# Two-block transformer layer on one core: the row tiles placed 192 bytes past the weight pieces, modulo 256

## The chip, the cores and the metric

One NeuronCore of a Trainium2 chip runs the whole program. The metric is the device time of one execution in microseconds (us); the runs of the kernel before took 2258.59 to 2259.89 us, median 2259.46.

## What is computed

Two transformer blocks in float32, one after the other, on 256 tokens of width 2048. Nearly all arithmetic is in dense projections of the kind "activations times weight matrix":

```python
# block 1
h = rms_norm(x, mix_norm_g);  proj = h @ w_in
attn = nsa_attention(q, kv, gates, ...)        # compressed, selected and window branches
conv = conformer_conv(conv_in, ...)            # GLU, 31-tap depthwise conv, LayerNorm, swish
x = x + concat([attn, conv]) @ w_out
x = x + conv_glu_ffn(rms_norm(x, ffn_norm_g), w_up, ffn_conv_w, ffn_conv_b, w_down)
x = rms_norm(x, final_norm_g)
# block 2
ada = silu(c) @ w_ada + b_ada                  # six modulation vectors
z = (rms_norm(x) * (1 + scale_m) + shift_m) @ w_in_2
o = concat([mla_mixer(...), gla_mixer(...)]) @ w_out_2
x = x + gate_m * rms_norm(o)
f = (silu(h @ w_ffn_gate) * (h @ w_ffn_up)) @ w_ffn_down   # h: modulated rms_norm of x
return x + gate_f * rms_norm(f)
```

## The kernel before, in words

**Every projection is done as three products.** Weights and activations are float32, but the tensor engine is used in its float32r form. So each operand is split in a rounded high part and the remainder as a low part, and the product is taken as high*high + high*low + low*high. The activations are kept transposed, 128 channels on the partitions and 256 tokens along the row; such a 128 x 256 piece, and its low part, are what is called **rows** here. The weights stream in from memory: a DMA brings 1 MB into `raw`, ScalarE writes the high part into a `wh` buffer, VectorE the low part into a `wl` buffer (`split_h`, `split_l`, lines 456 to 475). There are four `wh` and three `wl` buffers of 128 x 1024 elements (4096 bytes per partition), cut into pieces of 128 x 128 (512 bytes per partition).

**The matmuls** are issued by `run_group` (line 551). In most groups (mode "w") a weight piece is the stationary operand and the rows move: per piece and channel block three matmuls of 256 columns, (high weights, high rows), (high weights, low rows), (low weights, high rows), each with a weight load of its own. In groups of mode "x" the rows are stationary, in slices of 128 tokens, and 512 weight columns move. In the profile the two operands of a matmul stand after the arrow, the moving one first: "X,wh" is a matmul of mode "w", "wh,hid" one of mode "x".

**Where rows live.** `xsrc` gives the main rows: the high parts `XH` (16 blocks at a distance of 384 elements) and the low parts `XL` (16 blocks of 256) in one tile `X`. Other groups read: `o` (attention output, two times 8 blocks), `ch` and `cl` (convolution output, high and low), `hid` (hidden rows of both feed-forward stages), `cqs`, `ckh`, `ckl` (the compressed queries and keys of the second block), and `oh0`..`oh7`, `ol0`..`ol7` (its attention output, which reuse the space of the `qn` and `kn` tiles). `rows()` (line 707) makes the tiles `X`, `o` and `hid`, and before the change it skips `PHASE` = 4 elements, 16 bytes, at the front of each.

**Where a tile lies** follows from the order in which tiles are asked for in a pool, and of the pools: each takes its size, rounded up to 32 bytes per partition. The pool `cp` (`setup`) comes first with `XT`, `adaT`, `gf`, `X`, `vecs`, `kc`, `cs`, `gs`; then `rp` (nine tiles of 1024 bytes), the three `raw` buffers of 8192 bytes, the seven `wh` and `wl` buffers, and behind them the pools of each stage (`b1`, `f1`, `b2o` with `b2`, `f2`).

**The order of the work** is written by a small model of the engines in the kernel: `run_group` issues a group's matmuls and, between them, work of other engines and small matmuls from generators (`side`, `tick`) when the model holds them to be due. Neither addresses nor paddings enter this model. One such generator is `ada_gen`, which now and then puts eight small float32 matmuls and one transpose between the row matmuls.

All compute instructions are issued by one wrapper and so show as line 305 in the profile; they are told apart by the names of their tiles.

Of the kernel before, what the change touches and what calls it, by code (L numbers as in the profile page):

```python
# [13 lines left out]
F32 = mybir.dt.float32  # L14
F32R = mybir.dt.float32r
# [8 lines left out]
T = 256  # L24
# [122 lines left out]
WARM = 8  # L147
SQ = 1
AHEAD = 2
PHASE = 4  # L150
XROW = 384
GROUPS, MCS, TILES, WLEN = make_plan()

# [26 lines left out]
class Layout:  # L180
    def __init__(self, items):
        self.at, o = {}, 0
        for k, n in items:
# [12 lines left out]
CB = Layout([("perm", 128), ("selA", 128), ("selB", 128), ("cm3", 384), ("glam", 128), ("rmask", 256), ("invf", 1),  # L196
             ("sgn", 1), ("wgu", 512)])
# [175 lines left out]
class Kern:  # L373
# [330 lines left out]

        self.act(self.kc[:, 3:4], self.eps, AF.Sqrt)

    def rows(self, pool, name, parts, skip=PHASE):


        t = pool.tile([128, skip + sum(n * w for n, w in parts)], F32R, name=name)  # L710
        out, o = [], skip
        for n, w in parts:
            out.append(t[:, o:o + n * w].rearrange("p (k t) -> p k t", t=w))
            o += n * w
        return out
# [48 lines left out]
    def setup(self):  # L764
        a = self.a
        self.XT = self.cp.tile([128, 16, T], F32, name="XT")
        self.adaT = self.cp.tile([128, 96], F32, name="adaT")
        self.gf = self.cp.tile([128, 16], F32, name="gf")
        self.XH, self.XL = self.rows(self.cp, "X", ((16, XROW), (16, T)))
        self.vecs = self.cp.tile([128, VEC.n], F32, name="vecs")  # L770
        self.kc = self.cp.tile([128, 4], F32, name="kc")
        self.cs = self.cp.tile([128, 16], F32, name="cs")
        self.gs = self.cp.tile([128, 16], F32, name="gs")
        self.v.memset(self.kc[:, 0:1], EPS)
        self.v.memset(self.kc[:, 1:2], 1.0)
        self.v.memset(self.kc[:, 2:3], float(np.pi / 2))
        self.eps, self.one, self.hpi = self.kc[:, 0:1], self.kc[:, 1:2], self.kc[:, 2:3]
        self.ident = self.vec("ident", 0, 128)
        self.ones = self.vec("ones", 0, 128)
        self.begin(*(g["key"] for g in GROUPS if g["w"] == "w_in"))  # L780
        self.no_rows()


    def block1_setup(self):
        tc, a, ph = self.tc, self.a, self.ph
        self.p1 = ph.enter_context(ExitStack())
        P = self.b1 = self.p1.enter_context(tc.tile_pool(name="b1", bufs=1))
        self.oh, self.ol = self.rows(P, "o", ((8, T), (8, T)))
        self.cacc = [P.tile([128, 4, T], F32, name=f"cacc{b}") for b in range(2)]
        self.cat = P.tile([128, CA.n], F32, name="cat")  # L790
        self.sy.dma_start(self.cat[:, :16], a["ca"][:, :16])
        self.cl = {}
        self.upad = P.tile([128, 8, 30 + T], F32, name="upad")
        self.kz = P.tile([128, 4, 2, T], F32, name="kz")
        self.V = P.tile([128, 2, 2, 4, 64], F32, name="V")
        self.Gt = P.tile([128, 2, 8, 2, 3], F32, name="Gt")
        self.cbias = P.tile([128, 2, 8, 2, 16], F32, name="cbias")
        self.kcz = P.tile([128, 4, 16], F32, name="kcz")
        self.vz = P.tile([128, 4, 64], F32, name="vz")
        self.qT = {}  # L800
        self.pe1 = self.p1.enter_context(ExitStack())
        Ep = self.early = self.pe1.enter_context(tc.tile_pool(name="early", bufs=1))
        g = self.gp
        g.memset(self.upad[:, :, 0:30], 0.0)
        g.memset(self.kz, 0.0)
        g.memset(self.kcz, 0.0)
        g.memset(self.vz, 0.0)
        g.memset(self.cbias, NEG)
        for i in range(4):
            self.evac[f"c{i}"] = lambda ps, i=i: self.ev_conv(i, ps)  # L810
            self.evac[f"q{i}"] = lambda ps, i=i: self.ev_q(i, ps)
        for i in range(8):
            self.evac[f"oa{i}"] = lambda ps, i=i: self.ev_add([2 * i, 2 * i + 1], ps)
            self.evac[f"ob{i}"] = self.evac[f"oa{i}"]
            self.evac[f"oz{i}"] = lambda ps, i=i: self.ev_oz([2 * i, 2 * i + 1], ps)
        self.evac["kvc"] = self.ev_kvc
        self.evac["kk"] = self.ev_kk
        self.evac["gt"] = self.ev_gt
        self.evac["vv"] = self.ev_vv

        z = self.cacc[0][:, 0]
        self.v.memset(z, 0.0)
        o = self.bank()
        for _ in range(WARM):
            self.mm(o[:, :T], z[:, :128], z)
        self.free(o)
        for n, (c0, c1) in enumerate(((0, 2), (2, 4), (4, 8))):
            self.load_x(c0, c1)
            self.load_raw(n + 1)
        self.load_x(8, 12)  # L830
        g = lambda k: self.ca("mix_g", k)
        self.feed_raw(range(2), g)
        self.side(self.first_gen(g))
        self.conv_side = self.side(self.conv_gen(), low=True)
        self.side(self.bias_gen())
        self.ffn1_evacs()
        self.block2_evacs()
# [51 lines left out]
    def conv_gen(self):  # L889
        up, ca = self.upad, self.cacc  # L890
        for i in range(4):
# [14 lines left out]
                self.tt(up[:, 0:2, 0:T], ca[0][:, 0:2], ca[0][:, 2:4], OP.add)  # L906
            elif i > 1:
                self.tt(up[:, 0:2, 0:T], up[:, 0:2, 0:T], y, OP.add)
        self.ch = self.b1.tile([128, 8, T], F32R, name="ch", tag="ch")
        yield  # L910
        yield from self.need(1)
        o = self.sums([up[:, 0, 0:T], up[:, 1, 0:T]])
# [317 lines left out]
    def pre_u0_0(self):  # L1230
        self.idles = 0
        while "att" not in self.flags:
            self.idle()
        self.p1.close()
        self.p2 = self.ph.enter_context(ExitStack())
        P = self.f1 = self.p2.enter_context(self.tc.tile_pool(name="f1", bufs=1))
        self.begin("u0_0")
        self.side(self.norm_gen(lambda k: self.fv[:, 352 + k:353 + k]))
        self.hh, self.hl_ = self.rows(P, "hid", ((22, T), (22, T)))
        self.fv = P.tile([128, FV.n], F32, name="fv")  # L1240
        self.sy.dma_start(self.fv, self.a["fv"])
        self.vt = [P.tile([128, 4, 2 + T], F32, name=f"vt{i}") for i in range(2)]
        for t in self.vt:
            self.gp.memset(t[:, :, 0:2], 0.0)
        self.act(self.cs, self.vec("c", 0, 16), AF.Silu)
        self.ada_side = self.side(self.ada_first(P))
# [131 lines left out]
    def pre_z0(self):  # L1378
        self.drain(self.ada_side)
        self.p2.close()  # L1380
        P3 = self.p3 = self.ph.enter_context(ExitStack())
        Po = P3.enter_context(self.tc.tile_pool(name="b2o", bufs=1))
        self.b2o = Po
        self.qn, self.kn = ([Po.tile([128, T + PHASE], F32, name=f"{n}{h}")[:, PHASE:] for h in range(8)] for n in ("qn", "kn"))
        self.omh, self.oml = {}, {}
        self.gg = Po.tile([128, 128], F32, name="gg")[:, :16]
        self.p3i = P3.enter_context(ExitStack())
        P = self.b2 = self.p3i.enter_context(self.tc.tile_pool(name="b2", bufs=1))
        self.cbt = P.tile([128, CB.n], F32, name="cbt")
        self.sy.dma_start(self.cbt, self.a["cb"])  # L1390
        self.tt(self.gg, self.adaT[:, 32:48], self.vec("g_post", 0, 16), OP.mult)
        self.begin("z0", "z1")
        self.norm2_side = self.side(self.norm2_gen())
        self.cos = P.tile([128, T], F32, name="cos")
        self.sin = P.tile([128, T], F32, name="sin")
        self.qg = P.tile([128, 4, T], F32, name="qg")
        self.kg = P.tile([128, 4, T], F32, name="kg")
        self.sr = P.tile([128, 8, T], F32, name="sr")
        self.Vg = self.Vm = None
        self.krz = P.tile([128, 2, T], F32, name="krz")  # L1400
        self.zkr = P.tile([128, T], F32, name="zkr")
        self.dec = P.tile([128, 4, 4], F32, name="dec")
        self.kdz = P.tile([128, 3, 128], F32, name="kdz")
        for t in (self.krz, self.kdz):
            self.gp.memset(t, 0.0)
        self.side(self.rope_gen())
        self.ada_side = self.side(self.ada_late(P))
# [76 lines left out]
        self.side(self.rms_gen(c, 4, "g_q", self.cqh, self.cql))  # L1484

    def ev_shift(self, dst, ps, scales=(1, 1, 1, 1)):
        sh = self.b2.tile([128, 4], F32, name="sh", bufs=2)
        for e, (d, p, s) in enumerate(zip(dst, ps, scales)):
            self.shift(sh[:, e:e + 1], p, s)
            self.tt(d, p[:, :T], self.R, OP.mult)  # L1490
        for e, (d, s) in enumerate(zip(dst, scales)):
            self.act(d, d, AF.Identity, bias=sh[:, e:e + 1], scale=s)
# [129 lines left out]
    def mla_gen(self, h):  # L1622
# [27 lines left out]
        while self.pt_busy:  # L1650
# [17 lines left out]
        self.mm(o[:, 128:T], self.Vm[:, 1, hs], PT[:, 256:], False, True)  # L1668
        self.pt_busy = False
        yield  # L1670
        oh, ol = (self.b2o.tile([128, T + PHASE], F32R, name=f"{n}{h}", tag=f"{t}{h}")[:, PHASE:]
                  for n, t in (("oh", "qn"), ("ol", "kn")))
        self.omh[h], self.oml[h] = oh, ol
        self.act(oh, o[:, :T], AF.Copy)
# [354 lines left out]
```

## Time and profile before

| | us |
|---|---|
| median of 3 runs (2258.59 to 2259.89) | 2259.46 |
| the profiled execution | 2265.83 |
| its span, first to last instruction | 2263.9 |
| TensorE busy (PE) in it | 2234.7 |
| weight loads (PEld) | 2137.7 |
| VectorE (DVE) | 1698.5 |
| ScalarE (ACT) | 1187.7 |
| mean granted clock of TensorE, of full speed | 0.996 |

The profiled execution took 6.37 us more than the median run. Busy times are the union of an engine's instructions. Matmuls overlap each other in the records (one starts before the end of the one before it), so how fast they follow is read from how many of them stand in a stretch, not from the mean length of one.

### The profile page before, as it was taken

Reading aid. Unit: us, or ns where it says so; the run is one execution under the profiler, and the core shown is the slowest. Engines: PE = TensorE matmul, PEld = TensorE weight load, DVE = VectorE, ACT = ScalarE, POOL = GpSimd, SP = SyncE. Lnnn points to the kernel's source line nnn. Section 1 sums busy time; section 2 is a strip of 40 time slices with the busy share of each in tenths; the row PEclk is TensorE's granted clock in tenths of the full one; section 3 lists DMA queues with packets and bytes.
Section 4 is the critical chain, followed back from the end, with each engine's and each line's share of the span. In section 5 each row is a group of like instructions: output and inputs, shape, how many; then the busy total and the mean of one; then the engine's idle time right before and its main releaser. Section 6 shows DMA issues by size and latency. Waiting matters only on the chain.

```text
span 2263.9 us, 42338 instructions
## 1 busy us (share of the span) xinstructions
PE 2234.7 (99%) x17486; PEld 2137.7 (94%) x17486; DVE 1698.5 (75%) x2632; ACT 1187.7 (52%) x1826; POOL 4.9 (0%) x16
## 2 busy tenths in 40 slices
PE   8999999999999999999999999999999999999997
PEld 8998889999999999999999889989998999889996
DVE  7999888898987788888879876577665665544455
ACT  5447776655553355555556664555444444444443
POOL 0000000000000000000000000000000000000000
PEclk9999999999999999999999999999999999999999
DMA  6544325688888787877756644546666665555553
GB/s 242 186 166 159 127 80 193 239 293 301 303 287 308 294 297 284 301 291 290 251 204 225 214 153 148 193 149 215 241 239 231 246 236 192 187 183 171 187 186 130
DMA packets 89089, 499.22 MB, mean 221 GB/s; under 512 B 9904, under 2 KB 12352, under 8 KB 42432
## 3 DMA queue, kind: packets, MB, share of 16 engines
q1 hardware_dynamic: 88896, 496.51, 61.7%
q8 instruction: 137, 2.24, 0.4%
q14 instruction: 56, 0.46, 0.1%
HBM read 494.35 MB, written 2.12 MB: 219 GB/s over the span
## 4 chain that ended last, share of the span: by engine, by line
PE 93%; DVE 4%; ACT 2%; issue 1%; DMA 1%; SPq 0%; DVEq 0%; ACTq 0%
PE ps L305 93%; DVE wl L305 1%; DMA raw<-in_wst_dram 1%; DVE cacc L305 0%; ACT wh L305 0%; DVE og L305 0%; ACT P L305 0%; DVE X L305 0%; ACT X L305 0%; ACT L305 0%; DVE ss L305 0%; DVE blk L305 0%; ACT y L305 0%; ACT vt L305 0%; DVE XT L305 0%
## 5 line engine op out<-in xcount | busy, mean ns | idle before, releaser
L305 PE MATMUL ps<-X,wh 128*128 128x256 f32 (+1 forms) x7680 | 1374.8, 281 | 3.6 <-ACT X L305 2.9
L305 ACT ACTIVATE wh<-raw 128x1024 fp32r<-128x1024 f32 (+2 forms) x741 | 781.5, 1056 | 875.6 <-PE ps L305 798.8
L305 DVE TENSOR_TENSOR wl<-raw,wh 128x1024 fp32r<-128x1024 f32 (+2 forms) x741 | 898.5, 1216 | 451.4 <-PE ps L305 381.3
L305 PEld LDWEIGHTS ps<-X,wh 128*128 128x128 f32 x7680 | 1174.5, 188 | 12.3 <-issue 5.8
L305 PE MATMUL ps<-X,wl 128*128 128x256 f32 (+1 forms) x3840 | 1073.8, 280 | 3.4 <-DVE wl L305 3.4
L305 PEld LDWEIGHTS ps<-X,wl 128*128 128x128 f32 x3840 | 721.3, 188 | 4.0 <-DVE wl L305 4.0
L305 DVE SCALAR_TENSOR_TENSOR ac<-wa,cs,ac 128x512 f32<-128x512 f32 x360 | 269.6, 749 | 6.4
L305 PE MATMUL ps<-hid,wh 128*128 128x256 f32 x1408 | 247.8, 279 | 0.0
L305 PE MATMUL ps<-wh,hid 128*128 128x512 f32 x704 | 220.1, 394 | 0.0
L305 PEld LDWEIGHTS ps<-hid,wh 128*128 128x128 f32 x1408 | 214.1, 188 | 1.2 <-issue 1.2
L305 PE MATMUL ps<-hid,wl 128*128 128x256 f32 x704 | 196.0, 278 | 0.0
L305 PEld LDWEIGHTS ps<-wh,hid 128*128 128x128 f32 x704 | 131.7, 188 | 29.2 <-issue 0.2
L305 PE MATMUL ps<-wl,hid 128*128 128x512 f32 x352 | 138.1, 392 | 0.0
L305 PEld LDWEIGHTS ps<-hid,wl 128*128 128x128 f32 x704 | 132.2, 188 | 0.0
L305 DVE SCALAR_TENSOR_TENSOR cacc<-upad,cat,cacc 128x256 f32<-128x256 f32 x240 | 99.7, 478 | 0.3 <-ACT cacc L305 0.2
L305 PEld LDWEIGHTS ps<-wl,hid 128*128 128x128 f32 x352 | 67.1, 191 | 15.7
L305 DVE SCALAR_TENSOR_TENSOR y<-vt,fv,y 128x256 f32<-128x256 f32 x176 | 73.4, 479 | 0.0
L305 PE MATMUL ps<-wh,X 128*128 128x512 f32 x192 | 62.0, 404 | 0.0
L305 PE MATMUL ps<-o,wh 128*128 128x256 f32 x256 | 48.9, 290 | 1.2 <-ACT o L305 1.1
L305 ACT ACTIVATE y<-ps,fv 128x256 f32<-128x256 f32 x84 | 49.0, 583 | 0.0
L305 ACT ACT_TABLE_LOAD x30 | 38.5, 1283 | 10.8 <-DMA XT<-in_x_dram 4.5
L305 PEld LDWEIGHTS ps<-wh,X 128*128 128x128 f32 x192 | 35.4, 189 | 7.3
(319 smaller groups left out, 1754.8 us busy)
## 6 DMA issues: line engine op xcount, KB each, us to landing
raw<-in_wst_dram SPq DMA_DIRECT2D x363, 1024.0 KB, 4.9
wa<-in_wada_dram SPq DMA_DIRECT2D x176, 512.0 KB, 6.2
wa<-in_wada_dram SPq DMA_DIRECT2D x32, 256.0 KB, 5.5
raw<-in_wst_dram SPq DMA_DIRECT2D x4, 768.0 KB, 4.4
raw<-in_wst_dram SPq DMA_DIRECT2D x4, 512.0 KB, 6.3
B<-dtab SPq DMA_DIRECT2D x8, 256.0 KB, 5.2
out_dram<-og SPq DMA_DIRECT2D x8, 256.0 KB, 2.8
XT<-in_x_dram SPq DMA_DIRECT2D x3, 512.0 KB, 7.5
```

The source lines that it names most:

```text
L305: return f(*x, **k)
```

## The change

The constant `PHASE` is replaced by `SKIP` = 48 elements (192 bytes), which `o` and `hid` now skip, while `X` skips nothing; in `setup` the tiles `X` and `vecs` are asked for after `kc`, `cs` and `gs`. `ch` is asked for at the start of `block1_setup`, behind `cacc`. `gg` is made 192 bytes long and put ahead of `qn` and `kn`, which lose their skip (and so do `oh` and `ol`). `cbt`, `dec` and `sh` are made longer, with only their first part used. No instruction is added, removed or moved to another place in an engine's order.

```diff
--- before.py
+++ after.py
@@ -147,7 +147,7 @@
 WARM = 8
 SQ = 1
 AHEAD = 2
-PHASE = 4
+SKIP = 48
 XROW = 384
 GROUPS, MCS, TILES, WLEN = make_plan()
 
@@ -704,7 +704,7 @@
 
         self.act(self.kc[:, 3:4], self.eps, AF.Sqrt)
 
-    def rows(self, pool, name, parts, skip=PHASE):
+    def rows(self, pool, name, parts, skip=0):
 
 
         t = pool.tile([128, skip + sum(n * w for n, w in parts)], F32R, name=name)
@@ -766,11 +766,11 @@
         self.XT = self.cp.tile([128, 16, T], F32, name="XT")
         self.adaT = self.cp.tile([128, 96], F32, name="adaT")
         self.gf = self.cp.tile([128, 16], F32, name="gf")
-        self.XH, self.XL = self.rows(self.cp, "X", ((16, XROW), (16, T)))
-        self.vecs = self.cp.tile([128, VEC.n], F32, name="vecs")
         self.kc = self.cp.tile([128, 4], F32, name="kc")
         self.cs = self.cp.tile([128, 16], F32, name="cs")
         self.gs = self.cp.tile([128, 16], F32, name="gs")
+        self.XH, self.XL = self.rows(self.cp, "X", ((16, XROW), (16, T)))
+        self.vecs = self.cp.tile([128, VEC.n], F32, name="vecs")
         self.v.memset(self.kc[:, 0:1], EPS)
         self.v.memset(self.kc[:, 1:2], 1.0)
         self.v.memset(self.kc[:, 2:3], float(np.pi / 2))
@@ -785,8 +785,9 @@
         tc, a, ph = self.tc, self.a, self.ph
         self.p1 = ph.enter_context(ExitStack())
         P = self.b1 = self.p1.enter_context(tc.tile_pool(name="b1", bufs=1))
-        self.oh, self.ol = self.rows(P, "o", ((8, T), (8, T)))
+        self.oh, self.ol = self.rows(P, "o", ((8, T), (8, T)), SKIP)
         self.cacc = [P.tile([128, 4, T], F32, name=f"cacc{b}") for b in range(2)]
+        self.ch = P.tile([128, 8, T], F32R, name="ch")
         self.cat = P.tile([128, CA.n], F32, name="cat")
         self.sy.dma_start(self.cat[:, :16], a["ca"][:, :16])
         self.cl = {}
@@ -906,7 +907,6 @@
                 self.tt(up[:, 0:2, 0:T], ca[0][:, 0:2], ca[0][:, 2:4], OP.add)
             elif i > 1:
                 self.tt(up[:, 0:2, 0:T], up[:, 0:2, 0:T], y, OP.add)
-        self.ch = self.b1.tile([128, 8, T], F32R, name="ch", tag="ch")
         yield
         yield from self.need(1)
         o = self.sums([up[:, 0, 0:T], up[:, 1, 0:T]])
@@ -1236,7 +1236,7 @@
         P = self.f1 = self.p2.enter_context(self.tc.tile_pool(name="f1", bufs=1))
         self.begin("u0_0")
         self.side(self.norm_gen(lambda k: self.fv[:, 352 + k:353 + k]))
-        self.hh, self.hl_ = self.rows(P, "hid", ((22, T), (22, T)))
+        self.hh, self.hl_ = self.rows(P, "hid", ((22, T), (22, T)), SKIP)
         self.fv = P.tile([128, FV.n], F32, name="fv")
         self.sy.dma_start(self.fv, self.a["fv"])
         self.vt = [P.tile([128, 4, 2 + T], F32, name=f"vt{i}") for i in range(2)]
@@ -1381,13 +1381,13 @@
         P3 = self.p3 = self.ph.enter_context(ExitStack())
         Po = P3.enter_context(self.tc.tile_pool(name="b2o", bufs=1))
         self.b2o = Po
-        self.qn, self.kn = ([Po.tile([128, T + PHASE], F32, name=f"{n}{h}")[:, PHASE:] for h in range(8)] for n in ("qn", "kn"))
+        self.gg = Po.tile([128, SKIP], F32, name="gg")[:, :16]
+        self.qn, self.kn = ([Po.tile([128, T], F32, name=f"{n}{h}") for h in range(8)] for n in ("qn", "kn"))
         self.omh, self.oml = {}, {}
-        self.gg = Po.tile([128, 128], F32, name="gg")[:, :16]
         self.p3i = P3.enter_context(ExitStack())
         P = self.b2 = self.p3i.enter_context(self.tc.tile_pool(name="b2", bufs=1))
-        self.cbt = P.tile([128, CB.n], F32, name="cbt")
-        self.sy.dma_start(self.cbt, self.a["cb"])
+        self.cbt = P.tile([128, -(-CB.n // 64) * 64], F32, name="cbt")
+        self.sy.dma_start(self.cbt[:, :CB.n], self.a["cb"])
         self.tt(self.gg, self.adaT[:, 32:48], self.vec("g_post", 0, 16), OP.mult)
         self.begin("z0", "z1")
         self.norm2_side = self.side(self.norm2_gen())
@@ -1399,7 +1399,7 @@
         self.Vg = self.Vm = None
         self.krz = P.tile([128, 2, T], F32, name="krz")
         self.zkr = P.tile([128, T], F32, name="zkr")
-        self.dec = P.tile([128, 4, 4], F32, name="dec")
+        self.dec = P.tile([128, 64], F32, name="dec")[:, :16].rearrange("p (h n) -> p h n", h=4)
         self.kdz = P.tile([128, 3, 128], F32, name="kdz")
         for t in (self.krz, self.kdz):
             self.gp.memset(t, 0.0)
@@ -1484,7 +1484,7 @@
         self.side(self.rms_gen(c, 4, "g_q", self.cqh, self.cql))
 
     def ev_shift(self, dst, ps, scales=(1, 1, 1, 1)):
-        sh = self.b2.tile([128, 4], F32, name="sh", bufs=2)
+        sh = self.b2.tile([128, 32], F32, name="sh", bufs=2)
         for e, (d, p, s) in enumerate(zip(dst, ps, scales)):
             self.shift(sh[:, e:e + 1], p, s)
             self.tt(d, p[:, :T], self.R, OP.mult)
@@ -1668,7 +1668,7 @@
         self.mm(o[:, 128:T], self.Vm[:, 1, hs], PT[:, 256:], False, True)
         self.pt_busy = False
         yield
-        oh, ol = (self.b2o.tile([128, T + PHASE], F32R, name=f"{n}{h}", tag=f"{t}{h}")[:, PHASE:]
+        oh, ol = (self.b2o.tile([128, T], F32R, name=f"{n}{h}", tag=f"{t}{h}")
                   for n, t in (("oh", "qn"), ("ol", "kn")))
         self.omh[h], self.oml[h] = oh, ol
         self.act(oh, o[:, :T], AF.Copy)
```

## Rows read from the trace of the kernel before

**Rows 1.** The page, parts 1 and 2: PE's share, the granted clock.

```profile
PE 2234.7 (99%) x17486; PEld 2137.7 (94%) x17486; DVE 1698.5 (75%) x2632; ACT 1187.7 (52%) x1826; POOL 4.9 (0%) x16
...
PEclk9999999999999999999999999999999999999999
```

**Rows 2.** The page, part 4: the chain that ended last, by engine.

```profile
PE 93%; DVE 4%; ACT 2%; issue 1%; DMA 1%; SPq 0%; DVEq 0%; ACTq 0%
```

**Rows 3.** The page, part 5: matmuls that read rows, and the weight split.

```profile
L305 PE MATMUL ps<-X,wh 128*128 128x256 f32 (+1 forms) x7680 | 1374.8, 281 | 3.6 <-ACT X L305 2.9
...
L305 DVE TENSOR_TENSOR wl<-raw,wh 128x1024 fp32r<-128x1024 f32 (+2 forms) x741 | 898.5, 1216 | 451.4 <-PE ps L305 381.3
...
L305 PE MATMUL ps<-X,wl 128*128 128x256 f32 (+1 forms) x3840 | 1073.8, 280 | 3.4 <-DVE wl L305 3.4
...
L305 PE MATMUL ps<-hid,wh 128*128 128x256 f32 x1408 | 247.8, 279 | 0.0
L305 PE MATMUL ps<-wh,hid 128*128 128x512 f32 x704 | 220.1, 394 | 0.0
...
L305 PE MATMUL ps<-hid,wl 128*128 128x256 f32 x704 | 196.0, 278 | 0.0
...
L305 PE MATMUL ps<-wl,hid 128*128 128x512 f32 x352 | 138.1, 392 | 0.0
```

**Rows 4.** Busy time by stretch, PE alone: from:to length, PE busy (matmuls), clock, DMA, GB/s.

```profile
399.00:476.00 77.00, 77.00 (x652) 1.00 0.71 255
...
1540.00:1655.00 115.00, 115.00 (x973) 1.00 0.65 230
...
sum 515.00, PE 515.00; mean PE 64.38
```

**Rows 5.** The same view, other stretches.

```profile
478.50:1004.00 525.50, 524.86 (x4538) 1.00 0.82 297
...
sum 712.50, PE 711.86; mean PE 142.37
```

**Rows 6.** The same view, three neighbouring stretches of one stage.

```profile
967.00:1003.00 36.00, 36.00 (x311) 1.00 0.85 309
1008.00:1040.00 32.00, 32.00 (x285) 1.00 0.79 289
1043.00:1083.00 40.00, 40.00 (x345) 1.00 0.81 297
```

**Rows 7.** The same view: the stage that reads ch and cl.

```profile
352.00:388.00 36.00, 36.00 (x310) 1.00 0.56 197
```

**Rows 8.** The same view: stages with 512 weight columns moving.

```profile
1690.00:1735.00 45.00, 45.00 (x194) 1.00 0.69 243
...
2195.00:2240.00 45.00, 45.00 (x201) 1.00 0.48 165
```

**Rows 9.** Groups of instructions by line, 364 to 380 us, PE.

```profile
L305 PE MATMUL ps<-ch,wh 128*128 128x256 f32 x47 | 13.1, 279 | 0.0
L305 PE MATMUL ps<-cl,wh 128*128 128x256 f32 x46 | 12.9, 280 | 0.0
L305 PE MATMUL ps<-ch,wl 128*128 128x256 f32 x46 | 12.8, 278 | 0.0
```

**Rows 10.** Groups by line, 404 to 420 us and then 1014 to 1030 us, PE.

```profile
L305 PE MATMUL ps<-X,wh 128*128 128x256 f32 x92 | 16.4, 280 | 0.0
...
L305 PE MATMUL ps<-X,wh 128*128 128x256 f32 x60 | 10.2, 276 | 0.0
```

**Rows 11.** Timeline of PE around 1006 us: start, length, work, count.

```profile
1006.10 0.33 PE L305 MATMUL ps<-vecs,ac 128*128 128x128 f32 x1 [0.35 <-ACT ac L305]
1006.19 0.48 PE L305 MATMUL ps<-X,wh 128*128 128x256 f32 x2
```

**Rows 12.** One tile's instructions: what writes ol (eight places in SBUF).

```profile
L305 DVE TENSOR_TENSOR ol<-ps,oh x8: 398/418/425, 1273.7 to 1338.6; 128x256 fp32r<-128x256 f32 x8
```

**Rows 13.** Busy time by stretch, all engines: PE, PEld, DVE, ACT, POOL busy.

```profile
540.00:600.00 60.00, 60.00 (x523) 59.34 (x522) 54.83 (x76) 32.17 (x45) 0.00 (x0) 1.00 0.82 295
```

## The prediction

> **What bounds the kernel now.** I read the page first, then the chain, the costliest groups, and the busy time by stretch. PE is busy 99% of the span at a granted clock of 9 tenths or more in every slice, which is the 2.4 GHz level [rows 1], and 93% of the chain that ended last is PE's own [rows 2]. VectorE, the next engine, is busy 54.83 of 60 us in the heaviest of the long stages and DMA 0.82 of it [rows 13], so PE could be a few per cent faster before either ends last. The time is therefore the number of matmuls times the distance at which they follow each other. I call that distance the pitch. The mean length in the groups (281 and 280 ns, [rows 3]) is not the pitch, since records overlap; the pitch is the length of a stretch plus 0.28 us, by which the last record reaches over its edge, divided by the count.
>
> The reader is to see that the same instruction has three pitches. In one stage, with the same tiles X, hid, wh, wl, the same addresses and a clock of 1.00, three neighbouring stretches give 36.28/311 = 116.7 ns, 32.28/285 = 113.3 ns, and 40.28/345 = 116.8 ns [rows 6]. Elsewhere it is 77.28/652 = 118.5 ns [rows 4]. I call these fast (113.3), middle (116.7) and slow (118.6). At 2.4 GHz, 256 columns are 106.7 ns, so every matmul waits for 7 to 12 ns, and always for the same 7, 10 or 12. The steps are small parts of a matmul, no DMA or other engine in the trace has such a period, and the pitch flips at an interruption: the fast stretch begins behind one small matmul of the modulation vectors at 1006.10 us [rows 11]. I read this as two reading streams, the moving rows and the next weight piece, that meet in SBUF in a pattern which locks until something breaks it. Where they meet would depend on the distance of their addresses, which is what the change sets.
>
> **How the time is made up.** Slow: 515 us of row matmuls [rows 4]. Middle: 712.5 us [rows 5]. Fast: 32 us [rows 6]. With 512 weight columns moving: 45.39/194 = 234.0 ns in one stretch and 45.39/201 = 225.8 ns in another [rows 8], which is 117.0 and 112.9 per 256 columns, the middle and the fast pitch again. There are 704 + 352 such matmuls with hid [rows 3] and, by the code, 288 with X and 24 with ckh and ckl: 1,368, or 317 us. The rest: X and hid in mode "w" are 7680 + 3840 + 1408 + 704 = 13,632 [rows 3]; the slow stretches hold 515/0.1186 = 4,340, the middle 712.5/0.117 = 6,090, the fast one 285, so 2,920 are left, and the code gives 1,344 to o, ch, cl, oh, ol, cqs, ckh and ckl. These 4,260 I take at the pitch of the stretch with ch and cl, 36.28/310 = 117.0 ns [rows 7].
>
> **The change, part by part.** From the sizes in the code, from the start of X to the first wh buffer lie 40,992 + 1,856 + 32 + 64 + 64 (X, vecs, kc, cs, gs) + 9,216 (nine tiles of rp) + 24,576 (raw) = 76,800 bytes = 300 x 256, so the rows, 16 bytes into X, lie 16 bytes past the weights. After the change it is 40,960 + 1,856 + 9,216 + 24,576 = 76,608 = 299 x 256 + 64, and the rows start X: they lie 192 past. In the same way o and hid go from 16 to 192, ch from 0, cl from 32, oh and ol from 16, 48, .. 240 (32 more per head), cqs, ckh and ckl from 160, all to 192. So the change does what it says. All weight pieces also move by 32 bytes as a whole.
>
> Nothing is issued more or less: no DMA, wait or instruction, and no step passes another on SP's, POOL's or any other queue. ch is now claimed at the start, but its space was its own before, so no release is waited for. The DMA into cbt moves the same bytes. For VectorE and ScalarE the address seems of little account: the eight writes of ol, at eight distances, take 398 to 425 ns [rows 12], a spread of 7%; should it fall on the weight split (1216 ns, [rows 3]), it would be 85 ns of a step in which PE has 24 matmuls, 2.8 us, to do. That cover holds as long as PE is the bound. These parts cost nothing.
>
> What is left is the pitch, which no row shows at 192, so I bound it. Below: the fast pitch everywhere. Slow stretches 515 x (1 - 113.3/118.6) = 23.0, middle 712.5 x (1 - 113.3/116.7) = 20.8, the rest 4,260 x 3.7 ns = 15.8, the wide ones, without the 45 us that are fast, 272 x (1 - 225.8/234.0) = 9.5: 69 us less. Above: the slow pitch everywhere. Middle 712.5 x (118.6/116.7 - 1) = 11.6, fast 1.5, the rest 4,260 x 1.6 ns = 6.8, the wide ones 317 x 1.6% = 5: 25 us more.
>
> Between them I take the row that is nearest. 192 is a whole number of quarters of 256 bytes; of the tiles now read only ch (distance 0) lies so. That quarters are what counts is my choice; 176 and 208 of oh would be closer in bytes, but change at every third matmul and give no pitch of their own. Its matmuls run in turn with those of cl (distance 32), and records in that stretch are 279 and 278 ns long for ch, 280 for cl [rows 9]. On the scale of X at distance 16, where slow is 280 and fast 276 [rows 10], ch stands at the middle pitch and cl at the slow one. So I forecast that rows at a whole quarter settle at the middle pitch and leave the slow one: 515 x (1 - 116.7/118.6) = 8.3 us, and the rest 4,260 x 0.3 ns = 1.3 us, the wide matmuls and the middle stretches unchanged. The sum is 9.6 us less. Against the profiled execution, 2265.83 with 1.9 us around its span, that is 2256.2; the median run is 6.37 us quicker than the profiled one, and I put the difference on it: 2259.5 - 9.6 = 2249.9, or 2250.
>
> The Trainium skill, on the page "TensorE: Matmul & The Clock Gate", part 2, step 1 of the walk through a matmul, says that the engine has two independent read ports to SBUF, so that loading the next weights takes no read bandwidth from the running matmul. By that rule no distance matters and the time stays where it is; it is a rival below. The trace does not bear it out as it stands, since the pitch is above 106.7 ns by three different amounts at one and the same address pair. The same page's section on the back-to-back gap gives 262 cycles for 256 columns, 109 ns; if nothing met at all, an estimate from that page would be some 140 us less (8 ns on 13,632 + 1,344 + 2 x 1,368 times 256 columns).
>
> **The rivals.** *The streams no longer meet, or as seldom as they can.* The fast pitch exists [rows 6, 8], so it is a possible order of the two streams; a distance of three quarters of 256 could put the rows always behind the weights. Against it: at 16 bytes it holds for only 77 of the 1,500 us listed. 2259.5 - 69 = 2190.
>
> *Nothing changes,* because the lock is set by the instants at which instructions follow, not by addresses: the two neighbours in [rows 6] differ with the same addresses. Then the shares stay as they are: 2259.5.
>
> *Slower: the new distance holds the slow pattern.* Its place is the middle stretches, 712.5 us, above all the long feed-forward stage. Price 1.9 ns per matmul. It speaks for this that slow already takes two fifths of the stretches, and that the weight pieces themselves are moved by 32 bytes, the distance at which cl is slow. It decides once 4.5/0.0019 = 2,400 matmuls more are slow than leave it. If all are: 2259.5 + 25 = 2285.
>
> **How the numbers follow.** What a measurement of this kernel can tell from no change is about 0.2%, 4.5 us. Forecast, a middle pitch: 0.34, its own range 2241 to 2255. Fast everywhere or nearly: 0.20. No change: 0.16. Slower: 0.30. So faster 0.54, same 0.16, slower 0.30. The range reaches from the fast bound to the slow one, 2190 to 2286; a pitch below the fast or above the slow one is the 1 or 2 in 10 left out.
>
> **What would show it.** If I am right, the stretch from 399 to 476 us, slow now, has some 662 matmuls where it has 652 [rows 4], the stretch of ch and cl keeps 117, and no tile shows 118.6 for long. DVE, ACT and DMA busy times stay within a per cent. If the fast rival holds, these 77 us have 682 or more and all stages have one pitch; if the slow one, the modulation stage (478 to 1004 us) shows 118.6 or above. The forecast is wrong in kind if the pitches are new ones, or if PE's idle time grows, which would mean that an address slowed another engine.

## The result and the profile after

The changed kernel takes 2233.48 us, the median of 4 runs (2231.22 to 2238.19), against 2259.68 us before: ratio 0.9884, 95% interval 0.9865 to 0.9904. That is 26.2 us less, where 9.6 were forecast: the sign and the range hold, the size doesn't. The measured time lies between the forecast (2250) and the rival in which the streams no longer meet (2190).

The page of the changed kernel, parts 1, 4 and 5 (the profiled execution took 2238.19 us, its span 2236.3):

```profile
PE 2206.7 (99%) x17486; PEld 2109.8 (94%) x17486; DVE 1697.2 (76%) x2632; ACT 1186.6 (53%) x1826; POOL 4.9 (0%) x16
...
PE 93%; DVE 3%; ACT 2%; DMA 1%; issue 1%; SPq 0%; DVEq 0%; ACTq 0%
...
L305 PE MATMUL ps<-X,wh 128*128 128x256 f32 (+1 forms) x7680 | 1351.8, 280 | 3.0 <-ACT X L305 2.7
...
L305 DVE TENSOR_TENSOR wl<-raw,wh 128x1024 fp32r<-128x1024 f32 (+2 forms) x741 | 898.0, 1215 | 426.9 <-PE ps L305 365.3
```

Beside [rows 1 to 3]: the counts of instructions are the same, the weight split takes 1215 ns instead of 1216, and PE's busy time falls by 2234.7 - 2206.7 = 28.0 us. The span falls by 27.6. So all of the gain is TensorE's own, with the same instructions. The mean length of a matmul has moved by 1 ns (281 to 280), as lengths are not the pitch.

The same kernel, PE's busy time by stretch (from:to length, busy and matmuls, clock, DMA, GB/s):

```profile
352.00:388.00 36.00, 36.00 (x320) 1.00 0.57 193
399.00:476.00 77.00, 77.00 (x659) 1.00 0.72 263
660.00:694.00 34.00, 34.00 (x291) 1.00 0.85 319
734.00:767.00 33.00, 33.00 (x294) 1.00 0.80 297
...
2165.00:2210.00 45.00, 45.00 (x199) 1.00 0.52 180
```

With the 0.28 us of the edge, as in the prediction, the two neighbours at 660 and 734 us have 34.28/291 = 117.8 ns and 33.28/294 = 113.2. The stretch of ch and cl has 36.28/320 = 113.4, where it had 117.0 [rows 7], and the stretch at 399 us 77.28/659 = 117.3 with a small fast part at its ends, where it had 118.5 [rows 4]. The middle and the slow pitch of before (116.7, 118.6) are gone from the matmuls of 256 columns. Of the starts that could be sorted, in runs of twelve, 7,548 matmuls are at 113.3 and 5,028 at 117.8, with 492 between; before it was 504 at 113.3, 6,516 at 116.7 to 117 and 5,412 at 118.6. The mean over all matmuls, in 256 columns, goes from 117.2 ns to 115.3.

Which of the two it is changes where something else breaks in, as before. The timeline of PE in the changed kernel (start, length, work, count):

```profile
954.80 0.27 PE L305 MATMUL ps<-vecs,ac 128*128 128x128 f32 x1
954.83 0.48 PE L305 MATMUL ps<-X,wh 128*128 128x256 f32 x2
955.15 0.28 PE L305 MATMUL ps<-X,wl 128*128 128x256 f32 x1
955.27 0.39 PE L305 MATMUL ps<-X,wh 128*128 128x256 f32 x2
955.50 0.28 PE L305 MATMUL ps<-X,wl 128*128 128x256 f32 x1
```

From one wl to the next are three matmuls: 955.50 - 955.15 = 0.35 us, three times 113.3 ns plus rounding. It begins behind one small matmul of the modulation vectors, and some 300 row matmuls ahead of that one were at 117.8.

### The profile page after: what moved, and what is told of

The parts are those of the page before. It is cut to its first block, busy times and chain, and to the rows that moved or that the text cites. A ratio compares the mean times of both kernels' runs of the same rounds, so it can differ in the third digit from the quotient of the medians.

```text
span 2236.3 us, 42338 instructions
## 1 busy us (share of the span) xinstructions
PE 2206.7 (99%) x17486; PEld 2109.8 (94%) x17486; DVE 1697.2 (76%) x2632; ACT 1186.6 (53%) x1826; POOL 4.9 (0%) x16
## 4 chain that ended last, share of the span: by engine, by line
PE 93%; DVE 3%; ACT 2%; DMA 1%; issue 1%; SPq 0%; DVEq 0%; ACTq 0%
PE ps L305 93%; DVE wl L305 1%; DMA raw<-in_wst_dram 1%; DVE cacc L305 0%; ACT wh L305 0%; DVE og L305 0%; ACT P L305 0%; DVE ss L305 0%; DVE blk L305 0%; ACT L305 0%; ACT X L305 0%; DVE X L305 0%; DVE XT L305 0%; DVE P L305 0%; ACT ge L305 0%
## 5 line engine op out<-in xcount | busy, mean ns | idle before, releaser
L305 PE MATMUL ps<-X,wh 128*128 128x256 f32 (+1 forms) x7680 | 1351.8, 280 | 3.0 <-ACT X L305 2.7
L305 ACT ACTIVATE wh<-raw 128x1024 fp32r<-128x1024 f32 (+2 forms) x741 | 781.4, 1056 | 846.2 <-PE ps L305 795.6
L305 DVE TENSOR_TENSOR wl<-raw,wh 128x1024 fp32r<-128x1024 f32 (+2 forms) x741 | 898.0, 1215 | 426.9 <-PE ps L305 365.3
```

The costliest lines, as they stand in the source:

```text
L305: return f(*x, **k)
```

## The experiments

The theory was that the distance from weights to rows, modulo 256, sets the pitch. The rivals: the place of the weight pieces (also moved, by 32 bytes); what the other engines do beside PE; the instants alone.

**Row matmuls alone, sixteen distances.** Bursts of 60 matmuls, with one or more small matmuls between bursts (the loop, shortened to this mode):

```
for i in range(20):
    k, c = i % 2, slice(128 * (i % 8), 128 * (i % 8) + 128)
    ops = ((wh[:, c], R[:, k]), (wh[:, c], R[:, 2 + k]), (wl[:, c], R[:, k]))
```

> Only row matmuls of 256 columns, in bursts of 60, each burst behind a small float32 matmul; 16 distances of rows from weights (ra = 0, rb = 16, .. rp = 240 bytes) with the weights at 64 modulo 256 (names ending in x) and again at 32 (ending in y); no weight stream, no VectorE work beside it. Leaves out the whole computation of the reference. Theory distance: the pitch (busy time of a burst over its count) is set by the distance; 192 (rm) has bursts at 113.3 and 117.8 ns, 16 (rb) at 113.3, 116.7 and 118.7, and x and y agree. Rival place: x and y differ, the pitch goes with the absolute place of the rows or weights. Rival other engines: every distance runs at about 109 to 113 ns, since DMA, VectorE and ScalarE, which make the waiting, are still.

Measured, the pitch over the last 30 starts of each of six bursts (weights at 64; with weights at 32 it is the same but where more than one value stands):

```
distance   0      16           32           48     64     80         96     112
ns         120.0  116.7/118.7  116.7/117.8  118.3  117.8  118.2-120  120.0  113.3
distance   128        144          160          176    192          208    224    240
ns         118.7/120  116.7/118.7  117.3-120    119.3  113.3/117.8  119.2  118.3  117.2
```

The groups by line of this kernel (busy us of 360 matmuls, mean ns of one; g, h, m are the distances 96, 112, 192; x and y the weights at 64 and 32):

```profile
L68 PE MATMUL ps<-rgx,wh 128*128 128x256 f32 x360 | 44.5, 283 | 0.0
...
L68 PE MATMUL ps<-rmx,wh 128*128 128x256 f32 x360 | 43.1, 280 | 0.0
...
L68 PE MATMUL ps<-rhx,wh 128*128 128x256 f32 x360 | 42.5, 277 | 0.0
L68 PE MATMUL ps<-rmy,wv 128*128 128x256 f32 x360 | 42.4, 278 | 0.0
```

These busy times also hold each burst's beginning (its first two starts are some 200 ns apart) and its last record, so they rank the distances; the pitches above are read from the starts. The page of this run shows what else was at work:

```profile
PE 1429.2 (99%) x12096; PEld 1428.5 (99%) x12096; DVE 1.9 (0%) x2; ACT 65.1 (5%) x133; POOL 0.2 (0%) x4
```

With VectorE at 0% and 2 GB/s of transfers the whole spread from 113.3 to 120.0 is there. So the other engines don't make it; the distance does. At 192 both values of the changed kernel appear, but only with the weights at 64; with the weights at 32, where the changed kernel has them, all six bursts are at 113.3. At 16 two of the values of the kernel before appear. Distance 0 alone, without cl, has 120.0, as high as any in the map: the row from which the forecast was taken (ch, [rows 9]) said nothing like it, as every third matmul there read cl at 32.

**The same for 512 moving weight columns.**

> The same with the rows stationary and 512 weight columns moving (leaves out the computation likewise). Theory distance: per 512 columns 226.7 to 235 ns, the fast and the middle pitch doubled, and 192 no worse than 16. Rival other engines: about 216 ns everywhere.

Per matmul of 512 columns: 226.7 to 227.5 ns at 0, 226.7 or 233.3 at 16, 229.8 at 176, 228.9 at 192, 226.7 to 228.4 at 240, and 231.9 to 234.5 at the others, 112 among them. The two maps have no order in common: 112 is the best place for one mode and among the worst for the other. (The first two bursts, at 267 and 271 ns, ran at the start of the kernel and are left out.)

**The place of the weights apart from the distance.** Kernel before with the weights at 32, rows still 16 past them; kernel after with the weights at 64, rows still 192 past them. Each is one tile more, ahead of all others of the constant pool:

```
 (before)  +  self.cp.tile([128, 56], F32, name="pd")
 (after)   +  self.cp.tile([128, 8], F32, name="pd")
```

> The kernel before with 224 bytes of padding ahead of everything: weights at 32 modulo 256 as in the changed kernel, the rows still 16 bytes past them. Theory distance: no change, 2255 to 2265 us, pitches 113.3, 116.7 and 118.7 as before. Rival place: most of the gain is here already, 2235 to 2245 us, with pitches of 117.8.

> The changed kernel with 32 bytes of padding ahead of everything: weights at 64 modulo 256 as before, the rows 192 past them. Theory distance: the gain stays, 2228 to 2240 us, pitches 113.3 and 117.8. Rival place: back to 2255 to 2265 us.

Measured: 2260.2 us, ratio 0.9997 (0.9987 to 1.0006), and 2234.12 us, ratio 0.9871 (0.9843 to 0.99). In the medians the 32 bytes change nothing that can be told apart; the gain stays with the 192. One stretch of the first and two of the second:

```profile
399.00:476.00 77.00, 77.00 (x665) 1.00 0.73 266
```

```profile
352.00:388.00 36.00, 36.00 (x308) 1.00 0.56 187
399.00:476.00 77.00, 77.00 (x684) 1.00 0.74 272
```

Which pitch a stretch has is not the same. In the first, whose profiled execution (2254.85 us) is the lowest of its ten runs, the stretch at 399 us is at 77.28/665 = 116.2 ns, where the trace of before has 118.5 [rows 4], and some 2,800 of the sorted matmuls are at 113.3, where it has 504. In the second the stretch of ch and cl is slow (36.28/308 = 117.8) and the one at 399 us fast (77.28/684 = 113.0), the reverse of the changed kernel. So the distance gives the pitches that can occur, and the shares of one trace are not fixed by it; whether the 32 bytes or a difference between executions moved them here, one trace of each doesn't tell.

**A finer map.** Sixty-four distances in steps of 4 bytes, weights at 64, four bursts each.

> A kernel of row matmuls alone, as in the first of these runs (it computes none of the layer), with 64 distances in steps of 4 bytes. Distance theory: the pitch is a function of the distance modulo 256, so the multiples of 16 give again what the first map gave (113.3 ns at 112, 113.3 or 117.8 at 192, 120.0 at 96 and 0), and a few bytes either side of 112 the pitch either stays at 113.3 (a plateau) or leaves it at once. Rival, that a burst draws its pitch by chance at every distance: the four bursts of a distance differ from one another as much as the distances do, and 112 gives 117 or more in one of its four.

Measured around the two good places:

```
distance   104        108    112    116          120          |  184    188    192          196    200
ns         120/130    120.0  113.3  121.3-121.8  120.9-122.2  |  120.0  118.9  113.3/117.8  120.0  120.0
```

No plateau: 4 bytes either side cost 6 to 8 ns, and of the 64 distances only these two ever reach 113.3. All multiples of 16 came out as in the first map, and bursts of one distance mostly agree or take one of two values; chance alone is ruled out.

**All rows at 112.** The map promised 113.3 ns at all times. The weight pieces were moved on by 80 bytes:

```
-        h = self.wp.tile([128, 1024], F32R, name="wh", bufs=LA + 1)
+        h = self.wp.tile([128, 1088], F32R, name="wh", bufs=LA + 1)[:, 20:1044]
...
-        l = self.wp.tile([128, 1024], F32R, name="wl", bufs=LA)
+        l = self.wp.tile([128, 1088], F32R, name="wl", bufs=LA)[:, 20:1044]
```

> The changed kernel with the weight pieces moved 80 bytes on, so that every row lies 112 bytes past them, modulo 256; the rest is as it was. Distance theory: the matmuls of 256 moving columns go from 115.2 ns to 113.3 at all times, some 14,976 of them, 28 us less; those of 512 moving columns go from 230 ns to 233.3 (the second map at 112), 1,368 of them, 4.5 us more: 2211 us, and up to 2220 if a part comes back as waits on VectorE. No stretch of 117.8 is left. Rival, that the pattern is drawn at each interruption whatever the distance: again a mix of 113.3 and 117.8, and 2233 us. Rival, that TensorE's gain is now given back to the weight split and the transfers: pitch 113.3, but 2225 us or more, with PE idle beside it.

> The kernel with all rows at 112, but the hidden rows of the second block, which are stationary under 512 moving weight columns, at 240, where the second map had 227 to 228 ns against 233.3 at 112. Distance theory: 1,056 matmuls by 5.5 ns, some 6 us less than with all rows at 112: about 2205 us. Rival, that the last stage is bounded by the weight split or by transfers by then: no difference from all rows at 112.

> The changed kernel with the weight pieces moved 96 bytes on, so that every row lies 96 bytes past them, 16 bytes short of the kernel at 112. Distance theory: 120.0 ns for each matmul of 256 moving columns against 115.2, 14,976 by 4.8 = 72 us more, and 234.5 against 230 for the 1,368 wide ones, 6 us more, so about 2310 us, slower than the kernel before by 2%. Rival, that the pattern is drawn at each interruption whatever the distance: 2233 us.

Measured: 2296.15 us at 112 (ratio 1.0169, 1.0154 to 1.0184), 2295.46 with hid at 240 in the last stage (1.0166, 1.0149 to 1.0183), 2302.93 at 96 (1.0195, 1.0175 to 1.0216). The kernel at 96 is 7 us below the value worked out from the map, and slow as the map had it: 120.0 ns in nearly all of it. The one at 112 missed by 85 us, on the other side of the kernel before. Its stretches:

```profile
1600.00:1660.00 60.00, 60.00 (x503) 1.00 0.67 236
2130.00:2170.00 40.00, 40.00 (x345) 1.00 0.56 187
```

60.28/503 = 119.8 and 40.28/345 = 116.8 ns, at a granted clock of 1.00: the starts have 120.0, 118.3 and 116.7, never 113.3. PE is busy 2265.8 of its 2293.2 us, so no other engine holds it up. The distance modulo 256 is thus not all. The hidden rows at 240 have 231.7 ns per wide matmul, not 227 to 228, and 233.3 at 112: 1,056 x 1.6 = 1.7 us, of which 0.7 shows.

**Place, order of work or the other engines?** In this kernel the weights begin at 112, 16 bytes past a multiple of 32; in the maps they began at 32 or 64. Row matmuls alone again, with seven places of the weights, and with the order of the layer (one row under many column groups, a new PSUM tile for each three).

> Row matmuls alone once more (none of the layer is computed), to settle why the layer with all rows at 112 had 120.0, 118.3 and 116.7 ns where the row matmuls alone had 113.3. Seven places of the weight pieces (0, 16, 32, 48, 64, 112 and 128, modulo 256) by the distances 0, 16, 96, 112 and 192, six bursts each; 112 and 192 also in the layer's order of work (one row for many column groups, and a new PSUM tile for each group of three). Theory of places: the pitch depends on where the weights begin as well as on the distance; with weights at 112 the distance 112 gives 116.7 to 120.0 as in the layer, with weights at 32 and 64 it gives 113.3 as before. Rival, the order of work: with the same addresses the layer's order gives 116.7 to 120.0 at 112 and the first order 113.3. Rival, the other engines: 113.3 at 112 in both orders and at all places, so that what ruled it out in the layer is what VectorE, ScalarE and the transfers do beside it.

Pitch in ns of six bursts each (the values in the layer's order are those of the last two lines):

```
weights at           0            16           32     48         64           112        128
distance 0           120.0        116.7/118.2  120.0  118.3      120.0        118.3      120.0
distance 16          113.3-118.7  117.3/120.0  118.7  117.3/120  116.7/118.7  117.3/120  116.7/118.7
distance 96          120.0        120.0        120.0  120.0      120.0        120.0      120.0
distance 112         113.3        120.0        113.3  120.0      113.3        120.0      113.3
distance 192         113.3/117.8  113.3        113.3  113.3      113.3/117.8  113.3      113.3/117.8
112, layer's order   113.3        118.4/120.0  113.3  120.0      113.3        118.4/120  113.3
192, layer's order   113.3/117.8  113.3        113.3  113.3      113.3/117.8  113.3      113.3/117.8
```

The groups by line (busy us of 360; c and d are weights at 32 and 48; v is 112, w 192, x 112 in the layer's order):

```profile
L65 PE MATMUL ps<-qdv,wh 128*128 128x256 f32 x360 | 44.6, 285 | 0.0
L65 PE MATMUL ps<-qdx,wh 128*128 128x256 f32 x360 | 44.6, 286 | 0.0
...
L65 PE MATMUL ps<-qcv,wh 128*128 128x256 f32 x360 | 42.6, 278 | 0.0
L65 PE MATMUL ps<-qcx,wh 128*128 128x256 f32 x360 | 42.6, 278 | 0.0
L65 PE MATMUL ps<-qdw,wh 128*128 128x256 f32 x360 | 42.4, 277 | 0.0
L65 PE MATMUL ps<-qcw,wh 128*128 128x256 f32 x360 | 42.4, 278 | 0.0
```

The place decides, and the order of work doesn't. There are two cases: weights at a multiple of 32, where 112 always gives 113.3 and 192 gives 113.3 or 117.8 (12 of 48 bursts at 117.8, none of them with weights at 32); and weights 16 past one, where 192 gives 113.3 in all 36 bursts and 112 gives 118.4 to 120.0. A shift of both by 32, which the two kernels above tried, leaves the case as it is, and their medians showed nothing.

**Rows at 112 with the weights where they were.** The same distance by moving the rows of X, o and hid:

```
-        t = pool.tile([128, skip + sum(n * w for n, w in parts)], F32R, name=name)
-        out, o = [], skip
+        t = pool.tile([128, skip + 64 + sum(n * w for n, w in parts)], F32R, name=name)
+        out, o = [], skip + 44
```

> The changed kernel with the weight pieces left where they are (32 modulo 256) and the rows of X, o and hid moved on by 176 bytes, so that they lie 112 bytes past the weights; ch, cl, oh, ol and the query and key rows stay at 192. Theory of places: 113.3 ns for nearly all matmuls of 256 moving columns, 233 for those of 512, 2210 to 2220 us. Rivals (order of work, other engines): 116.7 to 120.0 ns as with the weights moved, about 2290 us.

Measured: 2222.27 us, ratio 0.9832 (0.9812 to 0.9853), 2 us above the expected range and 74 below the kernel with the same distance and the weights at 112. Two of its stretches with 256 columns and one with wide matmuls:

```profile
399.00:476.00 77.00, 77.00 (x684) 1.00 0.75 269
478.50:1004.00 525.50, 524.17 (x4655) 1.00 0.83 303
2140.00:2185.00 45.00, 45.00 (x195) 1.00 0.56 187
```

77.28/684 = 113.0 (a few small matmuls among the count bring it below 113.3): the stretch that was slow now has 32 matmuls more than in [rows 4], and the long middle one 4,655 instead of 4,538 [rows 5]. The wide ones pay, as the map said: 45.39/195 = 232.8 ns.

**Both moved on by 16 bytes, distance 192.** Weights at 48, rows at 240: the case in which 192 held 113.3 in every burst.

```
+        h = self.wp.tile([128, 1088], F32R, name="wh", bufs=LA + 1)[:, 4:1028]
+        l = self.wp.tile([128, 1088], F32R, name="wl", bufs=LA)[:, 4:1028]
...
+        out, o = [], skip + 4
...
+        self.ch = P.tile([128, 8 * T + 64], F32R, name="ch")[:, 4:4 + 8 * T].rearrange("p (k t) -> p k t", t=T)
```

(cacc with cl, and qn, kn with oh and ol, in the same way.)

> The changed kernel with the weight pieces and the rows both moved on by 16 bytes (weights at 48 modulo 256, rows at 240; the query rows cqs and the latent rows ckh, ckl stay, which leaves them at 176): the distance is still 192, but both begin 16 bytes past a multiple of 32, where the row matmuls alone had 113.3 ns in all 36 bursts at 192. Theory of places: 113.3 ns for nearly all of the 14,976 matmuls of 256 moving columns against 115.2 in the changed kernel, 28 us, of which the kernel with rows at 112 got 15 for X, o and hid (its wide matmuls lost some 3 of that); the wide ones keep about 230: 2210 us, between 2205 and 2220. Rival, that the distance alone decides: 113.3 and 117.8 mixed as in the changed kernel, 2233 us. Rival, that reads and writes off the multiples of 32 slow the split on VectorE: the wl split above 1216 ns and PE idle growing, above 2225 us.

> Matmuls of 512 moving weight columns with the rows stationary, alone (none of the layer is computed): weights at 32 and at 48 modulo 256, sixteen distances, six bursts each. Theory of places: the two maps differ, as they did for 256 columns; with weights at 32 the distance 192 has 228 to 231 ns (the changed kernel has 230.5) and 112 has 233.3 (the kernel with rows at 112 has 233.4). Rival, that wide matmuls know the distance alone: the two maps are the same within 1 ns at every distance.

Measured: 2210.8 us, ratio 0.979 (0.9776 to 0.9803), the fastest of all, and at the value expected. Its page and stretches:

```profile
PE 2174.0 (99%) x17486; PEld 2082.2 (94%) x17486; DVE 1695.3 (77%) x2632; ACT 1187.6 (54%) x1826; POOL 4.9 (0%) x16
...
L305 DVE TENSOR_TENSOR wl<-raw,wh 128x1024 fp32r<-128x1024 f32 (+2 forms) x741 | 897.7, 1215 | 403.6 <-PE ps L305 348.6
```

```profile
352.00:388.00 36.00, 36.00 (x320) 1.00 0.55 184
399.00:476.00 77.00, 77.00 (x684) 1.00 0.77 280
478.50:1004.00 525.50, 524.14 (x4660) 1.00 0.83 304
2120.00:2165.00 45.00, 45.00 (x200) 1.00 0.55 188
```

The split takes 1215 ns on data that begin 16 bytes off, so the rival of a slower VectorE falls. Of the runs of twelve 11,976 matmuls are at 113.3; none of the long stretches is at 117.8. The wide ones have 226.7 ns where I had written that they keep about 230. The map of wide matmuls agrees: with weights at 48 the distance 192 has 226.7 in all six bursts, with weights at 32 it has 228.9, and the maps differ by up to 7 ns at single distances (96: 227.2 against 234.5). It also gives 231.7 at 240 with weights 16 past a multiple of 32, which is what the hidden rows at 240 had measured.

## Why the prediction was right and where it failed

**The bound** was right. PE's busy time and the span fell together (28.0 and 27.6 us), and still do in the kernel at 2210.8 us, where VectorE ahead of the split still waits for PE in 348.6 of its 403.6 us of idle time.

**Two streams that meet by the distance of their addresses**: right as far as it went, since the map with no other engine at work shows it, and the rivals (instants alone, other engines, nothing changes) fell with it. Where a distance has two values, something other than the addresses still chooses between them. It was short of one thing: the place of the pair against multiples of 32 counts as well. The change happened to leave the weights at a multiple of 32 (64 before, 32 after), so the sum was not touched by that.

**The step that failed** is the choice of the row nearest to 192: "So I forecast that rows at a whole quarter settle at the middle pitch and leave the slow one". It had two parts, and both were wrong. The row was of ch at distance 0, which alone has 120.0 ns with weights at a multiple of 32, not 117; what [rows 7] shows is a mixture with cl at 32. And "a whole quarter" is no class: 0, 64, 128 and 192 have 120.0, 117.8, 118.7 to 120, and 113.3 or 117.8. Distances that differ by 4 bytes differ by up to 8 ns, so no row at another distance can stand for one that was not read; the bounds were all that the trace of before gave. That the sign came out right is luck: the chosen row by itself, 120.0 ns at distance 0, would have forecast a slower kernel. In place of 8.3 + 1.3 us from the slow stretches alone, all matmuls moved to two new shares: 0.6 at 113.3 and 0.4 at 117.8, a mean 1.9 ns lower over some 17,400 matmuls' worth of 256 columns, 33 us of TensorE's time. Of these 28 show in the profiled execution. Matched with the trace of before, the n-th matmul of one with the n-th of the other, the some 4,940 matmuls that stood at the slow pitch take 14.5 us less, where 8.3 + 1.3 were forecast; the some 6,600 at the middle pitch take 11.3 us less, and that term, "the wide matmuls and the middle stretches unchanged", was put at nothing. The first 1,000 matmuls take 0.4 us longer, not 2 us less; the remaining 2.6 us are spread over later stages and were not followed further. PE at the start of the profiled execution, by stretch:

```profile
10.00:15.00 5.00, 1.85 (x14) 0.91 0.81 330
15.00:20.00 5.00, 4.83 (x22) 0.50 0.72 266
...
0.00:60.00 60.00, 55.03 (x382) 0.91 0.62 228
```

Behind a stretch in which PE was busy for 1.85 of 5 us its clock is at 0.50, the 1.2 GHz level, and over the first 60 us it is 0.91, where the profile of before has 0.97 and 392 matmuls. This execution is 4.7 us above the median of its kernel, so its start need not be that of them all.

**The check that nearly came true for the wrong reason**: the stretch from 399 to 476 us was to have some 662 matmuls and has 659. But its pitch is the new 117.8 with a fast part at its edge, not the middle one; the stretch of ch and cl, which was to keep 117, shows the difference (113.4). The text named that sign beforehand: "the pitches are new ones". The count was a weak sign in any case, since the kernel before with its weights at 32 has 665 there without the change.

**The edits costed at nothing** cost nothing: the split takes 1215 ns, the counts and the transfers are the same, and the 32 bytes by which the weights move as a whole made no difference to the median of either kernel. The rival in which they did make one, with cl's 32 bytes as its sign, fell with that. **The wide matmuls** were to stay: their mean with hid went from 231.2 to 230.3 ns, 1,056 x 0.9 = 1 us.

**The fast bound.** All matmuls at 113.3 was priced at 69 us. The kernel with weights at 48 has nearly that, and its profiled execution (span 2206.6) is 57.3 us below that of before; in medians it is 48.7. So the bound was of the right size; the change itself stops about half way (26.2 of 48.7 us), with 0.58 of the sorted matmuls fast, because of the place of its weights.

**The rule of independent ports.** In the row matmuls alone the same instructions took 113.3 to 120.0 ns at a clock of 1.00 with nothing but the place of the rows changed, so loading weights and reading rows do disturb each other. The Trainium skill, "TensorE: Matmul & The Clock Gate", part 2, step 1 has them independent; here the measurement decides. The Trainium skill's gap of 262 cycles, 109 ns, for 256 columns (same page, "Back-to-back issue gap") was reached in no run: the lowest is 113.3.

What stays open: why the good distances are 112 and 192, and why an interruption sets one pattern or the other. In the third map the same bursts, by their number, were at 117.8 in both orders of work, which speaks against mere chance. But with weights at 64 the first two maps have the second and third burst at 117.8 (the first map the fifth too) and the third map the first, fourth and sixth, so the small matmuls just ahead of a burst don't settle it; what does was not tried. Nor do the row matmuls alone show why the layer has 0.4 at 117.8 with weights at 32: there all 18 of their bursts at 192, in both orders of work, are at 113.3.

## What to carry to other kernels

When PE is the bound and its matmuls follow at more than their columns take, measure the pitch from the starts (or from counts in clean stretches, not from mean lengths), and look whether equal instructions have several pitches: then the addresses of the two operands are a setting to be searched. A map of row matmuls alone, over the distances in steps of 16 bytes and both places modulo 32, costs one small kernel and found here what no reasoning from rows at other distances did; it must have the places of the layer, for both modes, before its values are carried over, and they are then to be measured in the whole kernel (with weights at 32 and distance 192 the maps had 113.3 throughout, the layer a mixture). Fix the chosen place in the code for every tile that is read (weights at 48, rows 192 past them, modulo 256, took 2.1% off this kernel), since any later tile put ahead of them moves it.

## What the runs showed that was not expected

The pitch of a matmul of 256 moving columns goes from 113.3 to 120.0 ns over multiples of 16 bytes, in steps of 4 bytes it reaches 123.3, and 130.0 in two of four bursts at 104, with all else equal; that of 512 columns from 226.7 to 236.7. The two modes want different places: at 112 with weights at 32 the one has its best pitch (113.3), the other 233.3. With weights at 48 and rows 192 past them both have their best at once (113.3 and 226.7, twice 113.3).

The layer has the patterns of the row matmuls alone nearly everywhere, though VectorE is busy 76% of its time and 223 GB/s are moved beside it. Three things don't fit: 117.8 for 0.4 of the matmuls of the changed kernel, which the row matmuls alone never had with weights at 32; 113.3 for 504 matmuls of the kernel before (distance 16), and for some 2,800 with its weights at 32, which the row matmuls alone had in one burst with weights at 0 only; and 116.7 for some 2,000 matmuls of the kernel with weights and distance at 112, which no burst there showed.
